# A weight gradient by block products of pairs on one core: stores, the second slice's load, the last visit and the order of work are changed

## The chip, the cores and the metric

The kernel runs on one core of a Trainium2 chip. Its time is what the device measures for one execution, in microseconds: the median of three runs before the change is 161.35 us (161.24 to 161.46). One execution was also profiled.

## What is computed

```python
def reference(input, grad_output):          # (16, 512, 1024), (16, 512, 768), float32
    grad_weight = np.einsum('bmk,bmn->kn', input, grad_output)
    return grad_weight.astype(np.float32)   # (1024, 768)
```

Batch and m together are 8192 rows: the result is X^T G, X of 8192 x 1024 and G of 8192 x 768.

## The kernel before, in words

**Slices and pairs.** The 8192 rows are 64 slices of 128 rows. K is cut into two halves of 512 columns, each of four blocks q of 128, and N into two halves of 384 columns (LEFT, RIGHT). The first eight slices (`LOADS`, kind "s") are multiplied directly: four products A, B (left half of K by LEFT and RIGHT) and C, D (right half of K), each with four blocks q. The other 56 slices are taken in 28 pairs (kind "P", numbers 4 to 31): a pair is a 2 x 2 block product, done by seven products, A, B, C, 1, 5, 6, 7, in place of eight. Their operands are partly the data (A, 1, B, C), partly sums of halves in bf16 that VectorE makes (`sum_x`, `sum_g`, three stages each: tokens x0.u, x1.u, x2.u, g0.u, g1.u, g2.u). Every matmul is 128 x 128 stationary by 384 columns in bf16; there are 4 x (3 x 36 + 8 + 4 x 28) = 912.

**Loads.** Slices from the third on, and G from the second on, are loaded by GpSimd's software queue, which converts float32 to bf16 on the way. To begin early, X of slices 0 and 1 (`xf[0]`, `xf[1]`) and G of slice 0 (`gf`) come as float32 on the hardware queues of SP and ACT (lines 128 to 131) and are rounded to bf16 by VectorE and ACT (`round_by`, line 202). The roundings of G's right half and of slice 1 are tokens r0 to r4: r0 G RIGHT, r1 X columns 512 to 767, r2 X columns 0 to 255 (all on VectorE), r3 X columns 768 to 1023, r4 X columns 256 to 511 (on ACT).

**Visits.** PSUM has eight banks, and 32 blocks (p, q) are to be summed, so that most blocks visit a bank many times. "B0@2.1" opens a visit of block B0 in bank 2 with one matmul, "B0.3" goes on with three; "A0@R.1" uses the bank that A0, A1 or A2 holds for most of the run (5, 6, 7). A visit ends with a close: c by ACT (a copy, line 356), v by VectorE (a copy on the first visit, line 376, else bank plus the sum so far, line 378), k by VectorE with D folded in. "fB2@4" fills bank 4 with B2's sum so far by an ACT copy (line 309), and the matmuls add to it; a suffix s takes the sum from an aside. p and q are sums by GpSimd (line 388) in which a shared product is added.

**End.** A, B and C are finished by adding a shared product (line 371, or q by GpSimd), D by the last close of product 5, which does two sums (lines 364 and 366). Each of the 16 finished blocks of 128 x 384 is stored by `store` (line 291); with `HALVED = 4` the first four stores are cut in two halves each. A fill with two banks ("fB2@7+1") splits a visit in columns 0 to 255 in the first bank and 256 to 383 in the second; then `multiply` runs all its matmuls on the first part and then all on the second, and the last close does one sum and one store for each part, the first on SP's queue, the second on ACT's (lines 372 and 373). The order before has no such visit.

**Order.** `PLAN` is a list of such tokens in program order. Each engine takes its own instructions strictly in that order, and semaphores make it wait for its data and for its bank. SP issues the stores in the same order. Before TensorE's first real matmul, `WARMUP` runs matmuls on constants: one of 512 columns in bf16, two of 512 in float32, and fourteen of 128 columns in bf16.

Of the kernel before, what the change touches and what calls it, by code (L numbers as in the profile page):

```python
# [9 lines left out]
P = 128  # L10
# [4 lines left out]
    "C0@2.1 A0@R.1 r0 r1 r3 B1@1.1 r2 A2@R.1 r4 A1@R.1 vB1 A1.1 D3@4.2 A0.1 C0.1 D0@3.1 B2@0.1 cC0 B2.1 D0.1 "  # L15
    "fB1@1 A2.1 B3@2.2 cD3 B1.2 B3.1 D2@4.1 cB1 D2.1 vB3 D2.1 D0.1 A0.1 C1@2.3 C2@1.4 A1.2 cC2 B2.1 C1.1 B2.1 "
    "D2.1 cC1 D1@1.2 vD2 D1.1 fD3@2 D1.1 A2.2 cD0 vD1 B0@4.1 D3.2 A3@3.2 cD3 A3.2 B0.2 vA3 B0.1 C3@1.4 B2.2 "
    "B1@3.1 B0.1 cB2 B0.1 A1.2 cB0 D2@0.2 A0.3 D0@2.3 C3.2 A2.1 C0@4.1 vC3 C0.3 B1.2 B3@1.5 B1.1 D0.1 C0.1 vB1 "
    "C0.1 A0.2 vB3 D0.1 fD3@3 D2.2 vC0 fC3@1 A2.3 vD0 fD1@4 D3.3 vD2 D3.1 D1.1 g0.4 D1.1 fC1@0 D1.2 C3.1 fA3@2 "
    "g1.4 C3.1 C1.1 vD1 cD3 C1.3 kC3 fC2@3 A3.2 g2.4 A3.1 fB2@1 A3.1 x0.4 A3.1 C2.2 cA3 C2.1 x1.4 C2.2 A2.1 "  # L20
    "x2.4 10@2.1 cC2 A0.1 C1.1 v10 12@4.1 60@3.1 cC1 B2.1 g0.5 B2.1 c12 B2.1 61@0.1 g1.5 c60 62@2.1 B0@4.1 vB2 "
    "B0.1 c61 B0.1 11@3.1 c62 A1.1 vB0 A1.1 f12@1 A1.1 13@0.1 x0.5 13.1 12.1 11.1 c13 73@4.1 x1.5 73.1 c11 "
    "50@2.2 c12 k73 51@0.1 53@3.1 c50 53.1 x2.5 A1.1 52@4.1 g0.6 c53 52.1 51.1 fB1@2 A0.1 v52 63@1.2 c51 "
    "71@3.1 g1.6 71.1 fC0@4 g2.5 B1.2 g2.6 B1.1 c63 70@0.1 k71 70.1 C0.1 f10@1 C0.1 x0.6 C0.1 c70 B3@3.2 A1.1 "
    "cC0 10.1 x1.6 10.1 cB1 72@0.1 vB3 72.1 c10 72.1 C1@4.1 x2.6 f62@3 C1.1 60@2.1 k72 60.1 cC1 61@1.2 g0.7 "
    "A0.1 fB2@4 62.1 v61 62.1 B0@0.2 c62 g1.7 B2.2 vB0 c60 C3@1.2 cB2 C3.1 g2.7 C2@3.2 x0.7 fA3@2 C2.1 12@0.1 "
    "f51@4 12.1 vC3 A3.2 cC2 A3.1 v12 51.2 cA3 70@1.1 x1.7 70.1 c51 53@0.1 g0.8 53.1 A2.1 c70 A2.1 x2.7 A2.1 "
    "fB3@2 A1.1 v53 63@4.1 fB1@1 63.1 B3.1 g1.8 B3.1 f11@3 13@0.1 v63 13.1 cB3 B1.2 g2.8 11.1 v13 C3@4.1 cB1 "
    "C3.1 A2.1 x0.8 fC1@2s 11.2 C0@1.1 f71@0 C0.1 vC3 C1.2 cC0 71.1 x1.8 71.1 c11 71.1 vC1 52@1.2 c71 52.1 "
    "g0.9 A1.1 f73@3 60@4.2 v52 50@2.1 f62@0 50.1 g1.9 50.1 f13@1 73.1 v60 73.2 c50 62.1 x2.8 62.1 72@4.1 g2.9 "  # L30
    "72.1 c62 10@2.1 x0.9 10.1 c73 10.1 13.2 f70@0s v10 A0.2 f51@3 A0.1 v72 70.2 c13 51.1 x1.9 51.1 fC2@4s "
    "61@2.1 v70 61.1 fB2@1 61.1 C2.1 x2.9 C2.1 c51 B0@0.1 g0.10 B0.1 c61 B0.1 B2.1 vC2 B2.1 f11@3 B2.1 A2.1 "
    "vB0 f71@4 A3@2.2 x0.10 A3.1 cB2 11.1 A0.1 f12@0 11.1 g1.10 A2.1 71.1 f63@1 vA3 71.1 12.1 c11 12.1 g2.10 "
    "12.1 x1.10 c71 A1.2 g0.11 63.1 c12 63.2 fB1@4 x2.10 C1@3.2 g1.11 c63 62@2.2 vC1 B1.2 fB3@1 B1.1 v62 "
    "C0@0.1 fC3@3 C0.1 B3.1 g2.11 B3.1 cB1 B3.1 x0.11 C3.2 f72@4 C3.1 vC0 13@2.2 cC3 A2.1 x1.11 72.1 cB3 72.1 "
    "v13 72.1 f50@3s 73@0.2 g0.12 73.1 f53@1 52@2.2 v73 52.1 c72 50.2 g1.12 50.1 f60@0s 53.1 v52 53.1 fC0@4s "
    "53.2 g2.12 60.1 f51@2 v50 60.2 c53 A1.1 x0.12 A0.2 fB2@3 A1.1 C0.1 v60 f10@1 51.3 x1.12 C0.1 f70@0 10.2 "
    "vC0 c51 10.1 70.2 g0.13 70.1 f61@4s C2@2.2 x2.12 c70 C2.1 61.1 x2.11 c10 61.2 vC2 B2.2 f11@1 B2.1 g1.13 "
    "B0@0.1 f12@2 v61 B0.2 11.2 vB0 f62@4 11.1 12.2 cB2 x0.13 12.1 A3@0.1 c11 A3.2 g2.13 C1@3.1 f71@1 x1.13 "
    "C1.2 vA3 62.1 c12 62.2 g0.14 71.1 f63@0 71.2 x2.13 fC3@2 A2.1 63.1 vC1 63.1 c71 63.1 C3.1 g1.14 C3.1 c63 "  # L40
    "A2.1 g2.14 B3@1.1 c62 B3.2 x0.14 C3.1 A0.2 cC3 vB3 53@4.3 fB1@2 x1.14 73@0.2 v53 73.1 f72@1 50@3.2 x2.14 "
    "50.1 B1.1 v73 72.3 v50 60@4.2 c72 60.1 g0.15 B1.1 f52@0 B1.2 v60 13@3.3 A1.1 f70@4 x0.15 A1.2 cB1 52.2 "
    "v13 52.2 70.1 g1.15 70.1 c52 x1.15 70.1 A2.1 fC2@3 A2.1 g2.15 C0@0.1 g0.16 C0.1 c70 C0.1 C2.1 fB2@2 x2.15 "
    "C2.2 vC0 B0@4.2 cC2 B2.1 g1.16 B2.2 fC1@3 g2.16 51@1.2 vB0 51.1 cB2 12@0.2 x0.16 12.1 f10@4 C1.3 v51 10.2 "
    "cC1 10.1 x1.16 10.1 61@2.1 v12 61.1 c10 61.2 x2.16 f11@1 A1.1 71@0.1 g0.17 71.1 fB3@4 71.1 v61 62@3.3 v71 "
    "B3.3 v62 53@2.2 cB3 B1@0.1 g1.17 B1.1 11.1 v53 11.3 vB1 f60@2 A3@4.3 x0.17 c11 A3.1 A2.1 f72@3 A2.1 vA3 "
    "50@0.1 70@1.2 g0.18 72.1 f13@4 72.1 50.1 x1.17 50.1 72.1 v70 13.2 c72 13.1 g1.18 60.2 g2.17 c13 60.1 v50 "
    "63@1.1 fB2@3 63.2 g2.18 63.1 f73@0 A0.1 x0.18 A0.1 f52@4 A0.2 73.1 c60 x1.18 73.2 x2.17 73.1 52.1 x2.18 "
    "63.1 c73 C0@2.2 v63 C0.1 B0@0.2 vC0 B0.2 52.1 g0.19 52.1 fA3@2 A1.2 vB0 c52 B2.3 g1.19 f61@4 10@1.1 x0.19 "
    "10.2 A3.2 g2.19 51@0.2 x1.19 cA3 51.2 v10 cB2 A2.1 61.2 f62@2 v51 61.1 C1@3.2 x2.19 fC2@0 C1.1 62.1 g0.20 "  # L50
    "62.2 B1@1.1 vC1 B1.1 c62 C2.1 g1.20 B1.1 f53@3 A2.1 A1.1 g2.20 12@2.1 c61 vB1 12.3 f11@4 x0.20 C2.2 f70@1 "
    "C2.1 53.1 v12 53.1 cC2 53.2 x1.20 11.2 v53 A2.1 70.1 c11 70.1 x2.20 70.1 fB0@3 52@2.1 g0.21 52.1 B2@0.1 "
    "c70 B2.1 B3@4.1 g1.21 B3.1 v52 B3.2 B0.1 vB2 B0.1 C3@1.2 g2.21 C3.1 fC2@0 C3.1 vB3 C3.1 cB0 C3.2 A0.1 "
    "f72@2 A0.1 vC3 A0.1 13@4.1 C2.1 x0.21 13.1 f50@1 13.2 71@3.1 g0.22 71.2 x1.21 71.2 g1.22 72.3 g2.22 72.1 "
    "v71 50.2 c72 50.2 C2.1 x0.22 fC1@2 C2.1 13.1 A1.1 f60@3 A1.1 x1.22 A1.1 cC2 C1.2 v13 c50 C1.1 60.1 x2.21 "
    "60.1 cC1 60.1 x2.22 60.1 f63@0 60.1 C0@1.2 v60 C0.2 63.1 g0.23 63.3 vC0 A0.1 B0@3.1 c63 B0.1 g1.23 61@4.1 "
    "f51@1 61.2 x0.23 62@0.1 f11@2 62.1 51.1 vB0 51.3 x1.23 11.2 v61 11.2 61@3.1 A0.1 A2.1 v61 A2.2 62.1 v11 "
    "62.1 73@4.2 g0.24 f70@2 73.3 x2.23 c51 10@3.2 v62 10.1 fA3@1 10.2 x0.24 A1.2 70.2 x1.24 70.2 v10 50@0.3 "
    "x2.24 A3.2 v50 A3.3 v73 B1@3.1 fB3@0 B1.2 g2.23 cA3 B1.1 g0.25 B1.1 c70 B3.2 vB1 B3.1 f13@1 B3.1 12@2.1 "
    "g1.25 f53@4 12.2 x0.25 12.1 f52@3 12.1 53.2 vB3 53.2 x1.25 53.1 13.2 v12 13.1 52.1 g1.24 52.1 c13 52.1 "  # L60
    "g2.25 52.1 c53 52.1 x2.25 63@2.1 A0.1 f11@0 g0.26 63.2 B2@1.1 g1.26 11.2 v63 A2.2 B2.2 f60@2 x0.26 B2.2 "
    "c11 A0.1 B0@4.1 c52 B0.1 x1.26 B0.1 60.1 g2.24 fC2@0 60.1 g2.26 60.2 71@3.2 g0.27 c60 71.1 C2.2 x2.26 "
    "C2.2 vB0 C3@2.1 B2.1 A1.1 g1.27 fC0@4 A1.1 kC2 C3.3 g2.27 C3.1 f72@0 C0.2 x0.27 C0.3 vC3 71.3 kC0 72.1 "
    "fC1@2 72.2 vB2 72.1 fA3@4 72.2 x1.27 C1.2 c72 v71 C1.3 g0.28 f73@0 62@1.3 fB3@3 kC1 62.1 A0.1 73.1 g1.28 "
    "73.1 f51@2 v62 73.2 A3.1 g2.28 A3.2 x0.28 A3.1 52@1.2 cA3 51.1 x2.27 51.1 c73 51.1 x1.28 51.2 52.1 A1.1 "
    "50@0.1 v52 50.3 v51 61@4.1 f70@1 61.2 g0.29 61.2 70.1 g1.29 70.2 v61 70.1 A2.1 A1.1 v50 B3.1 f63@4 12@2.2 "
    "x0.29 12.1 63.3 x1.29 A2.2 g2.29 A2.1 70.1 x2.28 63.1 A0.1 v12 A0.2 B3.1 k70 B3.2 B1@0.1 x2.29 B1.1 cB3 "
    "B1.1 g0.30 B1.1 c63 B1.1 10@2.2 x0.30 f60@4 10.4 vB1 60.2 53@3.1 g1.30 53.2 x1.30 53.2 g2.30 13@0.2 v53 "
    "13.2 60.2 g0.31 f72@3 A1.2 f11@1 v10 A0.1 A2.1 72.1 g1.31 72.1 f12@2 72.1 11.1 g2.31 11.1 x2.30 11.2 "
    "x0.31 11.2 A1.1 13.1 c11 13.1 x1.31 12.1 cA1 12.1 v13 12.1 A0.1 f62@1 A2.1 x2.31 10@6.1 p63 c12 72.1 60.1 "  # L70
    "v10 cA2 62.3 cA0 62.1 v60 63@7.1 f73@6 63.1 qA0 v62 A3@0.1 f70@4 A3.1 73.1 v63 73.1 f50@5 73.2 qA2 v72 "
    "70.1 f53@2 A3.1 50.1 v73 70.1 fC3@3 53.1 50.1 v70 f61@1 qA1 50.1 C3.2 v53 fC2@7 C3.2 fB3@6 C3.1 pA3 61.2 "
    "cC3 61.1 v50 C2.1 f71@4 C2.3 qC3 f51@3 C2.1 v61 71.2 cC2 71.1 vA3 71.1 fC0@1 B3.1 qC2 B3.1 v71 B3.1 fB1@7 "
    "51.2 vB3 f52@0 51.1 C0.1 pC1 C0.1 fB0@4 v51 C0.2 fB2@5 C1@2.4 vC0 B1.2 52.1 vC1 52.2 vB1 B2.3 v52 B2.2 "
    "B0.4 vB2 B0.2 vB0 "
).split()

WARMUP = [("b", 512), ("f", 512), ("f", 512)] + 14 * [("b", 128)]
PAIRS_HELD = 11
SUMS_HELD = 8  # L80
MERGED = 2
HALVED = 4
ASIDES = 7
# [5 lines left out]
def kernel(  # L89
# [6 lines left out]
    nc = tc.nc  # L96
    bf16 = mybir.dt.bfloat16
    f32 = mybir.dt.float32
# [242 lines left out]
    def close(engine, p, q, queue):  # L341
# [39 lines left out]
        if last(p, q) and not opened[p, q] and not (engine == "c" and p in "ABC"):  # L381
            closed.add((p, q))
# [66 lines left out]
```

## Time and profile before

| what | value |
| --- | --- |
| median of three runs | 161.35 us (161.24 to 161.46) |
| the profiled execution, its own time | 161.48 us |
| its span in the trace | 159.7 us |
| mean granted TensorE clock | 0.999 |
| TensorE (PE) busy | 154.6 us (97%) |
| VectorE (DVE) busy | 136.1 us (85%) |
| ScalarE (ACT) busy | 104.4 us (65%) |
| GpSimd (POOL) busy | 42.6 us (27%) |
| DMA mean, software queue's share of it | 209 GB/s, 90.7% of 16 engines' span |
| first real matmul, sixth, last (start) | 5.91, 7.70, 155.75 us |
| last store issued, landed | 156.70, 158.80 us |

The span is from the first instruction to the last; the time of the execution holds 1.8 us more around it. Busy times of one engine overlap with those of others, so that they do not add up. A line of a timeline gives start, busy time, engine, line of the kernel, operation, what it writes and reads, how many such instructions were merged, and in brackets how long the engine was idle before and what ended that. Queue q0 is GpSimd's software queue, q1 is SP's and q10 ACT's.

### The profile page before, as it was taken

The numbers are of one execution on the slowest core, as the hardware profiler recorded it, in microseconds if no ns is written. First come the engines' busy times: TensorE is split into PE (matmuls) and PEld (weight loads), VectorE is DVE, ScalarE is ACT, GpSimd is POOL, SyncE is SP. The second block draws the span as 40 slices with busy tenths as digits, with TensorE's granted clock in tenths as the row PEclk, the third lists the DMA queues.
The fourth block names the chain that finished last, engine by engine and source line by source line (L and its number), as shares of the span: only waits on it lengthen the run. The fifth ranks groups of instructions, "written<-read, shape, count | busy, mean of one in ns | idle before, by whom it ended". The sixth has DMA issues, their size and how long they took to land.

```text
span 159.7 us, 2734 instructions
## 1 busy us (share of the span) xinstructions
PE 154.6 (97%) x931; PEld 91.2 (57%) x931; DVE 136.1 (85%) x316; ACT 104.4 (65%) x243; POOL 42.6 (27%) x77
## 2 busy tenths in 40 slices
PE   8899999999999999999999999999999999999990
PEld 3456656556555565665656565656566565656560
DVE  0514169999999999999999999989999899999992
ACT  3445238999999999967867585563465472339930
POOL 7442222222212222221222221222222100006930
PEclk9999999999999999999999999999999999999999
DMA  5999999999999999999999999999999999940696
GB/s 171 297 212 211 214 216 212 213 213 212 213 213 211 214 212 213 214 211 214 213 214 212 214 213 214 212 211 213 213 211 219 208 214 213 213 81 0 196 353 239
DMA packets 12829, 33.40 MB, mean 209 GB/s; under 512 B 1424, under 2 KB 4624, under 8 KB 12816
## 3 DMA queue, kind: packets, MB, share of 16 engines
q0 software_dynamic: 9360, 28.64, 90.7%
q1 hardware_dynamic: 3168, 3.54, 6.6%
q10 hardware_dynamic: 288, 1.05, 1.7%
q8 instruction: 7, 0.11, 0.3%
q14 instruction: 6, 0.05, 0.1%
HBM read 58.72 MB, written 3.15 MB: 387 GB/s over the span
## 4 chain that ended last, share of the span: by engine, by line
PE 91%; DMA 4%; DVE 2%; issue 1%; ACT 0%; ACTq 0%; DVEq 0%
PE bank L331 91%; DMA xf<-in_input_dram 4%; DVE acc L371 1%; DVE macc L364 0%; DVE xp L202 0%; ACT macc L356 0%; ACTq L129 0%; DVE acc L378 0%; DVE acc L366 0%; DVEq L371 0%
## 5 line engine op out<-in xcount | busy, mean ns | idle before, releaser
L331 PE MATMUL bank<-gp,xp 128*128 128x384 bf16 x576 | 105.4, 326 | 0.7 <-DVE xp L202 0.6
L331 PEld LDWEIGHTS <-xp 128*128 128x128 bf16 x576 | 55.8, 98 | 39.1 <-DVE xp L202 1.0
L331 PE MATMUL bank<-ge,xe 128*128 128x384 bf16 x336 | 65.9, 326 | 0.0
L331 PEld LDWEIGHTS <-xe 128*128 128x128 bf16 x336 | 32.7, 98 | 22.3 <-DVE xe L184 0.6
L309 ACT COPY bank<-macc 128x384 f32<-128x384 f32 x69 | 32.6, 489 | 10.4 <-DVE macc L378 6.2
L356 ACT COPY macc<-bank 128x384 f32<-128x384 f32 x64 | 29.4, 484 | 10.4 <-PE bank L331 10.1
L378 DVE TENSOR_TENSOR macc<-bank,macc 128x384 f32<-128x384 f32 x56 | 30.5, 554 | 1.2 <-PE bank L331 0.9
L154 POOL DMA_DIRECT2D xp<-in_input_dram x30 | 15.9, 529 | 52.6 <-DMA xp<-in_input_dram 21.9
L309 ACT COPY bank<-acc 128x384 f32<-128x384 f32 x46 | 21.8, 485 | 11.5 <-DVE acc L378 8.9
L356 ACT COPY acc<-bank 128x384 f32<-128x384 f32 x44 | 20.7, 480 | 11.4 <-PE bank L331 11.1
L153 POOL DMA_DIRECT2D gp<-in_grad_output_dram x30 | 15.9, 531 | 38.4 <-PE bank L331 17.2
L378 DVE TENSOR_TENSOR acc<-bank,acc 128x384 f32<-128x384 f32 x42 | 22.8, 553 | 1.9 <-PE bank L331 1.9
L184 DVE TENSOR_TENSOR xe<-xp 128x1024 bf16<-128x1024 bf16 x28 | 19.3, 689 | 1.0 <-DMA xp<-in_input_dram 0.9
L194 DVE TENSOR_TENSOR ge<-gp 128x768 bf16<-128x768 bf16 x28 | 15.5, 552 | 0.2 <-DMA gp<-in_grad_output_dram 0.2
L376 DVE COPY acc<-bank 128x384 f32<-128x384 f32 x9 | 5.0, 555 | 8.9 <-PE bank L331 8.9
L186 DVE TENSOR_TENSOR xe<-xe,xp 128x512 bf16<-128x512 bf16 x28 | 11.8, 421 | 0.3
L188 DVE TENSOR_TENSOR xp<-xp,xe 128x512 bf16<-128x512 bf16 x28 | 11.5, 419 | 0.0
L196 DVE TENSOR_TENSOR ge<-gp,ge 128x384 bf16<-128x384 bf16 x28 | 9.9, 353 | 0.2
L198 DVE TENSOR_TENSOR gp<-ge,gp 128x384 bf16<-128x384 bf16 x28 | 9.8, 354 | 0.2
L388 POOL TENSOR_TENSOR acc<-acc,macc 128x384 f32<-128x384 f32 x7 | 6.8, 1003 | 0.5 <-ACT acc L356 0.5
L388 POOL TENSOR_TENSOR macc<-macc 128x384 f32<-128x384 f32 x1 | 1.0, 1042 | 18.0 <-DVE macc L378 18.0
L202 DVE CAST gp<-gf 128x192 bf16<-128x192 f32 (+1 forms) x2 | 0.6, 310 | 4.9 <-DMA gf<-in_grad_output_dram 4.9
(23 smaller groups left out, 41.2 us busy)
## 6 DMA issues: line engine op xcount, KB each, us to landing
xp<-in_input_dram POOLq DMA_DIRECT2D x30, 512.0 KB, 16.7
gp<-in_grad_output_dram POOLq DMA_DIRECT2D x30, 384.0 KB, 16.7
out_dram<-acc SPq DMA_DIRECT2D x12, 192.0 KB, 2.1
xf<-in_input_dram ACTq DMA_DIRECT2D x2, 512.0 KB, 4.9
out_dram<-acc SPq DMA_DIRECT2D x8, 96.0 KB, 1.7
gp<-in_grad_output_dram POOLq DMA_DIRECT2D x3, 192.0 KB, 6.4
xp<-in_input_dram POOLq DMA_DIRECT2D x2, 256.0 KB, 7.8
gf<-in_grad_output_dram SPq DMA_DIRECT2D x2, 192.0 KB, 4.1
```

What stands on the lines that cost most here:

```text
L153: nc.gpsimd.dma_start(out=gp, in_=G[rows, :].rearrange("(p m) n -> p m n", m=2))
L154: nc.gpsimd.dma_start(out=xp, in_=X[rows, :].rearrange("(p m) k -> p m k", m=2))
L184: nc.vector.tensor_sub(out=xe[:, 0:2, :], in0=x[:, 1::-1, :], in1=x[:, 3::-2, :])
L186: nc.vector.tensor_sub(out=xe[:, 2, :], in0=xe[:, 0, :], in1=x[:, 0, :])
L188: nc.vector.tensor_add(out=x[:, 1, :], in0=x[:, 2, :], in1=xe[:, 2, :])
L194: nc.vector.tensor_add(out=ge[:, 0:2, :], in0=g[:, 0:2, :], in1=g[:, 1::2, :])
L196: nc.vector.tensor_add(out=ge[:, 2, :], in0=g[:, 3, :], in1=ge[:, 0, :])
L198: nc.vector.tensor_add(out=g[:, 1, :], in0=ge[:, 2, :], in1=g[:, 2, :])
L309: nc.scalar.copy(out=tile_[:, at : at + c1 - c0], in_=src[:, c0:c1])
L331: nc.tensor.matmul(tile_[:, at : at + c1 - c0], stat, mov[:, c0:c1], start=fresh, stop=True, skip_group_check=True,)
L356: nc.scalar.copy(out=to, in_=b)
L378: nc.vector.tensor_add(out=to, in0=b, in1=to)
```

## The change

Five parts, in the words of the code:

- `HALVED` is 0: every store of a whole block is one transfer.
- X of slice 1 is loaded in four transfers of 256 columns (1 KB a row) in place of one (4 KB a row): columns 512 to 767 and then 0 to 255 on SP's queue behind both halves of `gf`, columns 768 to 1023 and then 256 to 511 on ACT's queue behind `xf[0]`.
- The first warm-up matmul writes bank 4, the others bank 7 (all wrote bank 7).
- `PLAN` is another order of the same 912 matmuls. It has 128 visits that open a bank (127 before), 119 closes by c (115), 117 fills (115), 128 closes by v (129), two p and six q (three and five). Its first and last lines are below. B2's last visit is "fB2@7+1", with 2 and then 5 matmuls, and its close is the last token.
- `close` may now end a prepared block by ACT and store it; the new order has no such close.

```diff
 PLAN = (
-    "C0@2.1 A0@R.1 r0 r1 r3 B1@1.1 r2 A2@R.1 r4 A1@R.1 vB1 A1.1 D3@4.2 A0.1 C0.1 D0@3.1 B2@0.1 cC0 B2.1 D0.1 "
...
-    "cC3 61.1 v50 C2.1 f71@4 C2.3 qC3 f51@3 C2.1 v61 71.2 cC2 71.1 vA3 71.1 fC0@1 B3.1 qC2 B3.1 v71 B3.1 fB1@7 "
-    "51.2 vB3 f52@0 51.1 C0.1 pC1 C0.1 fB0@4 v51 C0.2 fB2@5 C1@2.4 vC0 B1.2 52.1 vC1 52.2 vB1 B2.3 v52 B2.2 "
-    "B0.4 vB2 B0.2 vB0 "
+    "A0@R.1 C2@2.1 A3@3.1 A2@R.1 cC2 A1@R.1 vA3 C0@1.1 C1@0.1 vC1 r3 r0 r2 D2@4.1 r1 D2.1 vC0 B0@2.2 B1@0.2 "
+    "cB0 D1@1.2 r4 C3@3.3 D2.1 A1.1 cC3 A1.1 vD2 A2.1 cB1 A2.1 B3@2.2 fC1@0 B3.1 C0@3.2 fA3@4 C1.2 vC0 C1.1 "
...
+    "f72@6 61.1 qA2 61.1 v70 50.1 cA0 50.2 f52@0 v61 53.1 72.1 fB3@7 72.1 qC0 v50 72.2 fC3@3 52.2 B3.1 f71@5 "
+    "B3.1 v72 qA0 C3.1 fC2@2 C3.2 v53 C3.1 cB3 C3.1 71.1 f51@4 71.1 qB3 71.1 v52 cC3 71.2 C2.1 fB2@7+1 C2.2 "
+    "qC3 C2.1 v71 C2.1 fC1@0 51.2 vC2 fB1@3 51.1 C1.2 v51 fB0@6 C1.2 B1.2 B0.2 vB1 B0.3 vC1 B0.1 B2.2 vB0 B2.5 "
+    "vB2 "
 ).split()
-HALVED = 4
+HALVED = 0
-    nc.scalar.dma_start(out=xf[1], in_=X[P : 2 * P, :])
-
-    wps = psum.tile([P, 512], f32, name="bank7")
-    for dt, cols in WARMUP:
+    for engine, b in ((nc.sync, 4), (nc.scalar, 6), (nc.sync, 0), (nc.scalar, 2)):
+        cols = slice(b * P, (b + 2) * P)
+        engine.dma_start(out=xf[1][:, cols], in_=X[P : 2 * P, cols])
+
+    for n, (dt, cols) in enumerate(WARMUP):
         dtype = f32 if dt == "f" else bf16
+        wps = psum.tile([P, 512], f32, name="bank4" if n == 0 else "bank7")
         nc.tensor.matmul(
...
             if engine == "c":
                 assert carried or away
                 assert not final or p in "ABC"
+                assert (p, q) not in prepared or (final and carried and len(parts) == 1)
                 nc.scalar.copy(out=to, in_=b)
...
         if final and p in "ABCD" and engine == "v" and (len(parts) == 1 or p == "A"):
             store(p, q, 0, NH, queue)
-        if last(p, q) and not opened[p, q] and not (engine == "c" and p in "ABC"):
+        if final and engine == "c" and (p, q) in prepared:
+            store(p, q, 0, NH, queue)
+        if last(p, q) and not opened[p, q] and (engine != "c" or p not in "ABC" or (p, q) in prepared):
             closed.add((p, q))
```

## The prediction, as it was put on record

> **What bounds the kernel now.** I read the page's slices first, then the chain of waits in order of time, then the timelines of the first 16 us and the last 8 us, then the DMA rows of short windows and the landing time of each load.
>
> The slices (4 us each), three rows of busy tenths:
>
> ```profile
> PE   8899999999999999999999999999999999999990
> DVE  0514169999999999999999999989999899999992
> DMA  5999999999999999999999999999999999940696
> ```
>
> TensorE, VectorE and the DMA engines are all full from 20 us to about 138 us. No one engine can be relieved for a large gain; only edges and small stalls are left. The chain says whose edges:
>
> ```profile
> 7.70 80.68 PE bank L331 x493
> 88.38 0.03 issue
> 88.41 0.49 ACT macc L356
> 88.90 0.04 issue
> 88.94 64.87 PE bank L331 x397
> ...
> 156.12 0.56 DVE acc L371
> ```
>
> From 7.70 us on it is TensorE, with one eviction in between, and at the end one VectorE sum. Matmuls of 384 columns start 0.1625 us apart. I call "the line" 7.70 + 0.1625 x (k - 6) for the k-th of the 912: a TensorE that never waits after the 6th. The last matmul starts at 155.75, 0.85 us behind the line. That 0.85 is all that the middle can give back.
>
> The loads pace it too. By the landings, a new X pair arrives every 4.3 us, and the pair's first matmul follows after 0.1 to 2.2 us (pair 6: 34.22 and 34.3; pair 10: 51.75 and 51.8; pair 31: 142.53 and 143.2). A TensorE that starts earlier meets data that is not there.
>
> The head, in the timeline:
>
> ```profile
> 4.57 1.50 PE L136 MATMUL bank<-const-bfloat16-1.0 128*128 128x128 bf16 x14
> 5.91 1.17 PE L331 MATMUL bank<-gp,xp 128*128 128x384 bf16 x5
> 6.02 0.36 DVE L202 CAST gp<-gf 128x384 bf16<-128x384 f32 x1 [0.71 <-DMA gf<-in_grad_output_dram]
> 7.14 0.50 DVE L202 CAST xp<-xf 128x256 bf16<-128x256 f32 x2 [0.76 <-DMA xf<-in_input_dram]
> 7.55 0.55 DVE L376 COPY acc<-bank 128x384 f32<-128x384 f32 x1
> ```
>
> Warm-ups keep TensorE until 5.91, five matmuls of slice 0 follow, then it waits for slice 1's X (landed 7.12) and its rounding; the sixth starts at 7.70.
>
> The tail, timeline and DMA issues of the page:
>
> ```profile
> 155.55 1.13 DVE L371 TENSOR_TENSOR acc<-bank,macc 128x384 f32<-128x384 f32 x2
> 155.75 0.33 PE L331 MATMUL bank<-gp,xp 128*128 128x384 bf16 x1
> 156.12 0.91 SPq L291 DMA_DIRECT2D out_dram<-acc  x2
> out_dram<-acc SPq DMA_DIRECT2D x12, 192.0 KB, 2.1
> out_dram<-acc SPq DMA_DIRECT2D x8, 96.0 KB, 1.7
> ```
>
> Call T the end of the last matmul's streaming, 155.75 + 0.16 = 155.92. The last sum starts at T + 0.20, ends at 156.68 (T + 0.76), its store is issued at 156.70 and lands at 158.80 (T + 2.88); 0.91 us of closing work follows. Stores of 192 KB land 0.52 to 0.57 us apart (mean 0.535) from 152.9 to the end: the write stream is full.
>
> **The head after the change.** The new order has seven matmuls of slice 0 that need only the left half of g (A0 C2 A3 A2 A1 C0 C1), then D2 on slices 0 and 1, B0 twice, B1 twice, and D1 as the 14th. The warm-ups are the same, so the first again starts at 5.91 and the seventh at 6.89. On VectorE the eviction vC1 stands before the rounding r0 of g's right half. vC1 can start 0.36 us after its matmul (as 155.75 to 156.12), at 7.25; evictions follow at 0.465 us (the tail's sums), so r0 runs 7.72 to 8.08 (0.36, row above) and the eighth matmul starts at 8.13. The line has it at 8.02. Then r2 (X columns 0 to 255), r1 and vC0 come on VectorE, each behind the other, and D1 needs the bank that vC0 frees.
>
> So it matters when r2's quarter lands, second on SP's queue behind both halves of g and another quarter. How do queues share the engines? Two windows, 2.75 to 3.5 us and 5.25 to 6.5 us (queue; packets, MB, share):
>
> ```profile
> q10 hardware_dynamic: 54, 0.22, 71.6%
> q1 hardware_dynamic: 52, 0.08, 28.2%
> ...
> q10 hardware_dynamic: 73, 0.26, 56.0%
> q0 software_dynamic: 76, 0.12, 52.0%
> ```
>
> Packets alternate one for one, whatever their size (4096 against 1536 bytes). A whole X row is one packet of 4096 bytes; a quarter's is 1024. So against the software queue (137 ns a packet) slice 1 now moves 1 KB a turn on each of two queues instead of 4 KB on one. A 1536-byte packet takes 65 ns, one of 4096 bytes 159: by the straight line through both, 46 to 48 ns for 1024 bytes. The new transfers follow on their queues with pauses of 0.25 to 0.45 us (as between the two gf loads, and the two xf loads). Eight packets per engine and quarter, in turns: until 4.8 with the right half of g (0.065 + 0.046 = 0.11 us a turn), from 5.3 with the software queue (0.137 + 2 x 0.048 = 0.23 us a turn of three queues, 0.185 of two). ACT's first quarter is through at 5.0, SP's first at 6.4, ACT's second at 7.15, SP's second at 8.3, landing 0.2 to 0.4 later (as xf: data through 6.5, landing 6.55 to 7.12 over the engines): about 8.5. I take 8.5; ends 7.1 (as now) and 9.0 (every pause long). Then r2 starts at 8.5, r1 at 8.7, vC0 at 8.9, done 9.47, D1 at 9.53, **0.52 us behind the line** (0.1 to 1.0). The second issue on ACT (0.45 us) delays its table load from 1.67 to 2.1, done 3.4, before its first data at 4.22: nothing. SP's two more issues precede any store: nothing.
>
> [...]
>
> **The load stream.** 512 packets at 46 ns instead of 128 at 159 are 3.2 us of engine time, 0.2 us over 16 engines, and pauses before the software queue starts (5.25) leave some 0.1 us idle. All software loads come 0.3 us later (0.1 to 0.45). In the new order pair 31's first matmul is the 834th (835th now), on the line at 142.23; landing 142.53 + 0.06 + 0.3 puts TensorE at least 0.66 behind. Pairs 9 and 20 ask for 0.6. So the head's 0.52 is covered, and the end of the middle lies between 0.66 and that plus stalls of other kinds. Before had 0.15 (40.4 us) and 0.25 (88.9 us, the eviction in the chain); part of such stalls is absorbed by the wait for loads. I take 0.80, against 0.85 now: **-0.05** (-0.4 to +0.6). The counts of copies change by 4 more evictions and 2 more fills on ACT, 0.41 us each beside work on an engine busy 65%: nothing. VectorE has one eviction fewer.
>
> **The tail.** The last visit, B2, has 7 matmuls, each now one of 256 and one of 128 columns with a weight load each. The warm-ups are the row: 128 columns take 1.50/14 = 0.107 us. 256 columns lie between that and 0.1625; I take 0.11, by the streamed columns. Cost 7 x (0.11 + 0.107 - 0.1625) = **+0.38** (0 if 128 columns took a third of 0.1625; 0.75 if 256 took 0.1625).
>
> [...]
>
> VectorE meanwhile is free: after B1, C1 and B0 (sums at T - 2.3, T - 1.8, T - 1.3) it takes the 256 columns at T - 0.33 and the 128 at T + 0.20. The 384-column sum lasts 0.56, the smallest cast 0.23; I take 0.29 for 128 columns. The store of 64 KB goes out on ACT's idle queue: an unhindered 96 KB one took 1.64, of which data is 0.3; 64 KB, 1.57. It lands at T + 0.2 + 0.29 + 0.03 + 1.57 = T + 2.09, against T + 2.88: **-0.79** (-0.5 to -0.9). The 128 KB part, issued at T + 0.1, is down before that unless the write stream is backed up.
>
> Four stores fewer on SP: its 20 issues stood 0.49 us apart from 147.2 to 154.9 and held the stream at 204 GB/s until 152, against 366 after. In the new order the last seven whole stores become ready 0.4 to 0.6 us apart; the backlog of 0.2 us that the last store now carries is in the -0.79.
>
> **Sum.** Against the profiled execution: 161.48 - 0.05 + 0.38 - 0.79 = 161.02. Its time stands 0.13 above the median of the runs; from 161.35 the forecast is **160.9**.
>
> **Rivals.**
> *The quarters land early.* If the 1 KB packets are not held to one a turn, the head is 0.1 behind and loads come 0.1 late; TensorE ends 0.5 behind the line, -0.35, with the tail 160.6. Against it: the counts of the windows. Chance 0.15.
>
> *The middle takes it back.* In the new order 23 visits open a bank no more than 7 matmuls after its last user's (19 now, of which one stalled, 0.25), and VectorE is full. Two or three more stalls of 0.2 that loads do not absorb: 161.35 +- 0.25. Chance 0.22. With 0.05 for the tail's gain being eaten by backed-up writes (161.2).
>
> *Bank handovers on a late VectorE, slower.* The same place; it decides from five such stalls on: head 0.52 + 1.1 = 1.6 behind the line, +0.77 - 0.41: 161.7. For it: head and order leave VectorE no pause after 8 us. Against it: before, with as full a VectorE, had two. Chance 0.18.
>
> **Numbers.** Forecast 160.9 (160.7 to 161.1), chance 0.40; early quarters 0.15: faster 0.55. Same 0.27, slower 0.18; 0.2% (0.32 us) is about what a measurement here can tell from no change. The range takes in the early head with a free split, 161.35 - 0.4 - 0.8 = 160.15, and a late head with stalls, 161.35 + 0.6 - 0.1 = 161.85.
>
> **What would show it.** The eighth matmul near 8.1 and the 14th near 9.5; casts of r2 waiting for xf until 8.5; pair 31 landing near 142.8; the last seven pairs of matmuls 0.22 us a pair; last VectorE sum about 0.3 us, last landing near T + 2.1 on ACT's queue. I am wrong if the 14th starts at 9.1 or at 10, if 128 columns take 0.054, or if TensorE's idle time in the middle grows past 1 us.

## The result, and the profile after

The changed kernel takes 166.78 us (median of six runs, 164.77 to 167.44) against 161.31: 1.029 times as long, with an interval of 1.023 to 1.035. I had forecast 160.9 and a range up to 161.85. Its profiled execution is the longest of the six (167.44 us, span 165.6) and is compared below with the profiled 161.48 of before. That execution counts as a slow run, 1.6% above the fastest of the six, and the ratio leaves it out and goes by the means of the runs, 166.01 against 161.35. Its mean granted clock is 1.000; the other five, which left no trace, have 0.979 to 0.990.

The chain of waits of the changed kernel, in order of time (start, us, what):

```profile
0.78 2.31 PE bank L138 x3
3.09 0.04 issue
3.13 2.09 PE bank L138 x2
5.22 0.04 issue
5.26 0.28 PE bank L138
5.54 0.04 issue
5.58 0.28 PE bank L138
...
9.69 2.25 PE bank L333 x7
11.94 0.02 issue
11.96 0.56 DVE acc L379
12.52 0.28 DVE gp L204
12.84 148.76 PE bank L333 x907
161.60 0.02 issue
161.63 0.42 DVE acc L374
```

In the chain of before, the first 7 us belonged to a load. Here they belong to the warm-ups (line 138), one by one: each lasts 0.28, then 0.04 of issue, then the next. Two lines of the timeline say the same in bulk:

```profile
5.26 4.42 PE L138 MATMUL bank<-const-bfloat16-1.0 128*128 128x128 bf16 x14
...
9.48 2.44 PE L333 MATMUL bank<-gp,xp 128*128 128x384 bf16 x7
```

Fourteen warm-ups that took 1.50 us now take 4.42, and the first real matmul starts at 9.48 instead of 5.91. The seven real matmuls behind it take 2.44 us: they start 0.32 apart, twice the 0.1625 of before, and so do the next ones up to 16.3 us.

The account of TensorE, from the starts of its matmuls. The 19th starts at 16.30, where the line of the prediction has 9.81: 6.49 us behind. That is 3.57 of later start, 0.95 for six steps at 0.32, 1.28 of waiting before the eighth (r0 behind vC1), 1.67 for eleven more slow steps, less the 0.98 that the first matmul of before is ahead of the line. From the 19th to the end only 0.13 is lost. The end of the matmuls is then 161.71 against 155.92: 6.49 + 0.13 + 0.02 (the split) - 0.85 = 5.79 later (the pace, not rounded, is 0.16248). Nearly all of the loss lies before 16.3 us.

The tail, in the timeline of the last microseconds:

```profile
160.31 1.07 DVE L374 TENSOR_TENSOR acc<-bank,macc 128x384 f32<-128x384 f32 x2
...
160.76 1.88 SPq L293 DMA_DIRECT2D out_dram<-acc  x4
161.63 0.62 DVE L374 TENSOR_TENSOR acc<-bank,macc 128x256 f32<-128x256 f32 x2 [0.25 <-PE bank L333]
162.28 0.37 ACTq L293 DMA_DIRECT2D out_dram<-acc  x1
```

The last sum is short, as forecast (128 columns in 0.28), and ends at 162.25, T + 0.54 with T = 161.71. But SP issues its stores back to back, 0.49 apart, to the end, each landing 0.43 to 0.56 after the one ahead. ACT's small store, issued at 162.28, lands at 164.67, 2.4 us later: T + 2.96. Before it was T + 2.88.

### The profile page after: what moved, and what is told of

Its sections match the earlier page's. It is cut to its first block, busy times and chain, and to the rows that moved or that the text cites. A ratio compares the mean times of both kernels' runs of the same rounds, so it can differ in the third digit from the quotient of the medians.

```text
span 165.6 us, 2754 instructions
## 1 busy us (share of the span) xinstructions
PE 159.3 (96%) x938; PEld 93.2 (56%) x938; DVE 136.1 (82%) x316; ACT 107.3 (65%) x250; POOL 42.5 (26%) x77
## 2 busy tenths in 40 slices
DMA packets 12829, 33.40 MB, mean 202 GB/s; under 512 B 1424, under 2 KB 4752, under 8 KB 12816
## 4 chain that ended last, share of the span: by engine, by line
PE 96%; DVE 1%; issue 0%; DVEq 0%
PE bank L333 91%; PE bank L138 5%; DVE acc L379 0%; DVE acc L374 0%; DVE gp L204 0%; DVEq L449 0%
## 5 line engine op out<-in xcount | busy, mean ns | idle before, releaser
L333 PE MATMUL bank<-gp,xp 128*128 128x384 bf16 (+2 forms) x583 | 107.2, 330 | 0.9 <-DVE gp L204 0.9
L333 PEld LDWEIGHTS <-xp 128*128 128x128 bf16 x583 | 57.6, 99 | 40.1 <-issue 4.6
L333 PE MATMUL bank<-ge,xe 128*128 128x384 bf16 x336 | 64.9, 326 | 0.0
L311 ACT COPY bank<-macc 128x384 f32<-128x384 f32 x66 | 31.3, 488 | 11.0 <-DVE macc L381 6.8
L359 ACT COPY acc<-bank 128x384 f32<-128x384 f32 x50 | 23.3, 482 | 17.1 <-PE bank L333 17.0
L381 DVE TENSOR_TENSOR macc<-bank,macc 128x384 f32<-128x384 f32 x59 | 32.2, 554 | 2.4 <-PE bank L333 1.8
L311 ACT COPY bank<-acc 128x384 f32<-128x384 f32 (+2 forms) x52 | 24.6, 482 | 12.4 <-DVE macc L381 7.1
L381 DVE TENSOR_TENSOR acc<-bank,acc 128x384 f32<-128x384 f32 x40 | 21.9, 555 | 7.7 <-PE bank L333 7.3
L138 PE MATMUL bank<-const-bfloat16-1.0 128*128 128x128 bf16 (+1 forms) x15 | 4.3, 286 | 1.6 <-PEq L438 0.8
L138 PEld LDWEIGHTS <-const-bfloat16-1.0 128*128 128x128 bf16 x15 | 1.6, 109 | 4.8 <-issue 4.8
```

The costliest lines, as they stand in the source:

```text
L138: nc.tensor.matmul(wps[:, 0:cols], nc.const_aps.tensor(1.0, (P, P), dtype), nc.const_aps.tensor(1.0, (P, cols), dtype), start=True, stop=True,
L311: nc.scalar.copy(out=tile_[:, at : at + c1 - c0], in_=src[:, c0:c1])
L333: nc.tensor.matmul(tile_[:, at : at + c1 - c0], stat, mov[:, c0:c1], start=fresh, stop=True, skip_group_check=True,)
L359: nc.scalar.copy(out=to, in_=b)
L381: nc.vector.tensor_add(out=to, in0=b, in1=to)
```

## The experiments

Theory 1 after seeing this: the edit of the warm-up lines gives every warm-up a new PSUM tile in the same bank, and a new tile waits until the matmul that wrote the old one has ended (0.28 us, then 0.04 of issue, in the chain above). In the instruction list of the compiled kernel before, no warm-up waits; in that of the changed kernel each one from the third on does:

```
Matmult bank_86<-const-float32-1.0 128x512
Matmult bank_88<-const-float32-1.0 128x512 [waits PE_49]
Ldweights const-bfloat16-1.0
Matmult bank_90<-const-bfloat16-1.0 128x128 [waits PE_49]
```

Theory 2: the new order and the quartered load are a loss by themselves.

**e1_one_tile**, one tile ahead of the loop, all else changed:

```diff
-    for n, (dt, cols) in enumerate(WARMUP):
-        wps = psum.tile([P, 512], f32, name="bank4" if n == 0 else "bank7")
+    wps = psum.tile([P, 512], f32, name="bank7")
+    for dt, cols in WARMUP:
```

> The changed kernel with one edit: the warm-ups write one PSUM tile, allocated ahead of the loop, as before. Theory 1 (a tile per warm-up makes each warm-up wait for the one ahead; that costs the 3.6 us of later start and the half-speed matmuls until 16 us): fourteen warm-ups 0.107 us apart, first real matmul at 5.91, real matmuls 0.1625 apart from the first. Then the rest of the change shows: SP's second quarter lands at 9.8 as in the changed kernel, D1 (the 14th) starts near 10.8, loads 0.4 to 1.0 later than before: 162.0 to 162.8. Theory 2 (the new order and the quarters are the loss): still above 164.

Measured: 163.76 (162.67, 162.82, 164.71, 164.86) against 161.42 of before on the same chip, ratio 1.015 (1.008 to 1.021). The profiled execution is the 162.67. Its timeline:

```profile
4.57 1.29 PE L138 MATMUL bank<-const-bfloat16-1.0 128*128 128x128 bf16 x14
...
5.70 1.30 PE L333 MATMUL bank<-gp,xp 128*128 128x384 bf16 x7
...
7.91 0.77 PE L333 MATMUL bank<-gp,xp 128*128 128x384 bf16 x3 [0.92 <-DVE gp L204]
9.74 0.50 DVE L204 CAST xp<-xf 128x256 bf16<-128x256 f32 x2 [1.89 <-DMA xf<-in_input_dram]
...
10.09 1.15 PE L333 MATMUL bank<-gp,xp 128*128 128x384 bf16 x5 [1.41 <-DVE xp L204]
```

The warm-ups are quick again, real matmuls start at 5.70 at full speed, and the 14th starts at 10.76 as expected. Theory 1 holds for the largest part. The remaining 1.2 to 3.4 us are the rest of the change: VectorE's cast waits for the last quarter until 9.74, and TensorE with it.

**e2_before_tile_each**, the kernel before with only the reverse edit, and **e3_two_tiles**, the changed kernel with bank 4 kept for the first warm-up but one tile for the others:

```diff
+        if n < 2:
             wps = psum.tile([P, 512], f32, name="bank4" if n == 0 else "bank7")
```

> The kernel before with one edit: a new PSUM tile for each warm-up, the first in bank 4, the others in bank 7. Theory 1: warm-ups 0.32 us apart, first real matmul near 9.5, 0.32 us a matmul until about 16 us: some 5 us slower, 165 to 167. Theory 2: within 0.5 us of before.

> The changed kernel with two warm-up tiles, bank 4 for the first and one in bank 7 for all the others: bank 4 is kept, the tile per warm-up goes. Theory 1 (the new tile, not the bank): as the kernel with one tile, within 0.3 us. Rival (bank 4 itself costs, D2's visit there waits): the 165 of the changed kernel, or a stall at D2.

Measured: 165.08 (163.81 to 165.93), ratio 1.022 (1.017 to 1.028), and 162.92 (162.69 to 164.41). In e2 the fourteen short warm-ups start at 5.26 and the first real matmul at 9.48, as in the changed kernel; the matmuls are 0.32 apart to the 12th (13.0), there to the 19th (16.3). So the tile per warm-up alone costs the old kernel 3.6 us (by the means of the runs). Three runs of e3 take 162.69 to 162.93, as the two quick ones of e1 do (162.67, 162.82), so bank 4 is harmless.

**e4_two_short**, the changed kernel with two 128-column warm-ups, still a tile each:

```diff
-WARMUP = [("b", 512), ("f", 512), ("f", 512)] + 14 * [("b", 128)]
+WARMUP = [("b", 512), ("f", 512), ("f", 512)] + 2 * [("b", 128)]
```

> The changed kernel with 2 warm-ups of 128 columns instead of 14, still a tile each: warm-ups end near 5.9, so the later start is gone and only the half speed is left. Theory 1 with both halves: first real matmul near 5.9, still 0.32 us apart until 11 to 16 us, 163 to 165. Rival (only the delay counts, the speed comes by itself with the first matmuls): full speed before 8 us and the time of the kernel with one tile.

Measured: 164.42 (164.24 to 164.59). Theory 1 was wrong in its second half: matmuls run at full speed from 5.6 on. But they fall back to 0.32 from 11.7 to 14.9, after TensorE has stood idle from 8.5 to 10.3 for the quarter. Three stretches (each with its length, busy times and counts of PE, PEld, DVE, ACT and POOL, then the granted clock, which is the third value from the end):

```profile
5.00:11.40 6.40, 3.56 (x18) 1.58 (x18) 2.80 (x9) 2.20 (x6) 2.06 (x5) 1.00 1.12 224
11.50:14.80 3.30, 3.30 (x12) 1.59 (x11) 0.56 (x1) 1.75 (x4) 1.12 (x3) 0.50 1.11 218
15.00:20.00 5.00, 5.00 (x33) 3.00 (x32) 1.90 (x4) 2.46 (x6) 1.58 (x3) 1.00 1.09 216
```

In the trace's clock records the half speed lasts from 11.49 to 14.90, 3.41 us. Only one execution of each kernel left a trace. By my estimate 3.41 us at half clock lower the mean clock of such a run by 0.010; the four runs of e4 have 0.986 to 0.990 and the two of e1 near 164.8 have 0.985 and 0.987, so they probably all lost it, and e1's two near 162.7 (1.000 and 0.996) did not. So the late quarter cost a second time, by about 2 us (the distance between e1's two pairs), when TensorE lost its clock behind the pause. The length of the pause alone does not decide it: e9b, further down, lost the clock after 2.2 us (7.14 to 9.32), and e16 kept it after 3.1 us (6.71 to 9.81). What decides stays open.

**e5_one_load, e6_halved, e7_unsplit** take the other parts away in turn. e5 is e1 with one load, e6 is e5 with halves, e7 is e5 with one bank for B2:

```diff
-    for engine, b in ((nc.sync, 4), (nc.scalar, 6), (nc.sync, 0), (nc.scalar, 2)):
-        cols = slice(b * P, (b + 2) * P)
-        engine.dma_start(out=xf[1][:, cols], in_=X[P : 2 * P, cols])
+    nc.scalar.dma_start(out=xf[1], in_=X[P : 2 * P, :])
 # e6:  HALVED = 4          e7:  fB2@7 in place of fB2@7+1
```

> The changed kernel with one warm-up tile and X of slice 1 again as one load on ACT's queue: what is left of the change is the order, the whole stores and the split last visit. Theory 1 (warm-up tiles and quarters are all the loss): xf lands near 7.1, D2 starts near 7.9 to 8.1 and D1 near 9.1, loads as before, no second clock record below 1.0; last matmul ends 0.2 to 0.5 earlier than before, but the stores land one after another at 0.53 us and the last lands some 2.9 after it: 161.0 (160.8 to 161.3). Theory 2 (the order is a loss by itself): 161.8 or more.

> The kernel with one tile and one load, and the first four stores halved again. If the end is bound by how fast the last nine stores go out (0.5 us an issue, 0.53 a landing), four more issues at the front cost nothing as long as SP waits for its data between them: within 0.15 of the kernel without halving. Rival (SP's queue is behind from the first store on): 0.5 to 1.0 slower.

> The kernel with one tile and one load, with B2's last visit in one bank. In the changed kernel a 128-column matmul there takes 0.056 and the pair 0.165, so the split costs TensorE nothing. If the write stream sets the end, the split gains nothing either: within 0.15. Rival (the shorter last sum and store do shorten the end, as I forecast): 0.4 to 0.8 slower without the split.

Measured: e5 161.73, ratio 1.0016 (1.0008 to 1.0025); e6 162.53; e7 161.41, ratio 0.9996 (0.9988 to 1.0005). So one load in place of four is worth about 1 us against the quick runs of e1 and about 3 against the others (two chips, so only roughly), and e5 lies between its two theories. Halving costs 0.80 here against what I expected, and the split costs 0.32 where I had expected nothing and forecast a gain. Of the 0.32, the two profiled executions show 0.27 within the span: 0.20 at the end of the matmuls, as the clock is granted at 6.80 in e5 and 6.32 in e7 (the first matmuls run at 0.32), and 0.07 in the stores (last landing T + 2.94 and T + 2.87). The rest lies outside the span: the runs of e5 and e6 have 1.87 to 2.10 us there, those of e1, e7 and the changed kernel 1.72 to 1.85; what this 0.2 is stays open.

The span does not end with the last store's landing. SyncE then goes through waits on the semaphores of its transfers one after another (line 444 in before, 449 in the changed kernel), 0.06 us each and in the order of the program, and how many of them are left behind the last store's own differs from kernel to kernel: from the last landing to the end it is 0.91 us in before, 0.97 in the changed kernel, 1.15 in e7 and 1.34 in e6. This hides a gain: in e7 the matmuls end 0.39 earlier than in before (155.52 against 155.92) and the last store lands 0.41 earlier (158.39 against 158.80), but 0.24 of it goes on these waits.

**e8_before_quarters**, the kernel before with the four quarters:

> The kernel before with only the load of slice 1 in four quarters. Theory 1: the last quarter lands near 9.8, the sixth matmul (A1 on slice 1, columns 0 to 255) starts near 10.3 instead of 7.70, software loads 1.0 to 1.2 later; 163 to 164, and up to 166 where the pause makes TensorE lose its clock. Rival (the quarters are harmless in the old order): within 0.5 of before.

Measured: 165.48 (165.19 to 166.4), ratio 1.026 (1.023 to 1.028). The sixth matmul starts at 10.29, and the profiled execution lost the clock for 3.41 us (11.37 to 14.78). The other three have mean clocks of 0.990, 0.990 and 0.979, so they probably did too. The quarters are as bad in the old order.

**e9b_before_rows**, the kernel before with two loads of 64 whole rows on the two queues:

```diff
+    for engine, r in ((nc.sync, 0), (nc.scalar, 64)):
+        engine.dma_start(out=xf[1][r : r + 64, :], in_=X[P + r : P + r + 64, :])
```

> The kernel before with X of slice 1 in two loads of 64 whole rows (4 KB a row), one on SP's queue behind g and one on ACT's queue. Same two queues as the quarters, but packets of 4 KB. Theory 1 (one packet a turn, so the 1 KB packets are what delays the quarters): both halves land by 6.3 to 6.8, earlier than the single load's 7.1; the sixth matmul starts near 7.5, behind slice 1's g; software loads within 0.2 of before; 161.2 to 161.5. Rival (a second queue and more transfers are the loss): landing after 7.5 and 162 or more.

Measured: 163.58 (162.72 to 166.08). ACT's half landed at 6.63 as expected, SP's at 8.74. The packet size is not the whole reason.

**e11_before_whole** (the kernel before, `HALVED = 0`), **e12_order_alone** (e7 with `HALVED = 4`), **e13_best** (e7 with the loads of e9b, r0 moved ahead, stores of C1 and B0 on ACT):

> The kernel before with only HALVED = 0. Before, the last store waits for VectorE (issued at 156.70 behind a sum that ends at 156.68) and then lands 0.2 later than an unhindered one. Without halves the write stream is less behind: 0.1 to 0.25 faster, 161.2 to 161.4. Rival (whole stores are worth 0.8, as with the new order, where SP's issues ran back to back to the end): 160.7.

> The new order alone: one warm-up tile, one load, B2's last visit in one bank, the first four stores halved as before. With the split last visit, halving cost 0.8. If that is SP's issue pace (20 issues of 0.49 back to back, the new order's stores being ready later or more bunched), it holds here too: 161.9 to 162.3, the order alone a loss of 0.5 to 0.8 that the whole stores win back. Rival (halving costs only together with the split): 161.4.

> What the runs so far point to: new order, one warm-up tile, whole stores, B2 in one bank; X of slice 1 in two loads of 64 rows on the two queues; the rounding r0 of g's right half ahead of the evictions vA3 and vC1; the stores of C1 and B0 on ACT's queue. D2 starts near 7.1 and waits no more for r0. If loads and writes set the pace, nothing is left to win but 0.1 to 0.2 at the last store: 161.1 to 161.4. Rival (the head's 0.4 us and SP's issue pace still count): 160.6 to 161.0.

Measured: e11 161.77, ratio 1.0018 (1.0008 to 1.0027), slower by 0.33 and not faster; e12 161.79, ratio 1.0022 (1.0014 to 1.0031); e13 162.21. In e12 SP issues the last 16 of its 20 stores 0.49 apart without a pause from 149.5 on, and the last goes out at 156.95, 0.39 after the last sum (156.56). So e7 wins 0.38 by whole stores (on another chip), a little less than expected. Its parts are only roughly known: the profiled executions, the longest run of e12 and the shortest of e7, differ by more, 0.28 in the end of the matmuls and 0.67 in the stores (last landing T + 3.54 against T + 2.87), less 0.24 of closing waits. In e11 the last store goes out right behind the last sum, as before, so whole stores had nothing to win. It is slower, and 0.25 of the 0.33 are closing waits (1.16 us against 0.91); its profiled execution, the longest of its ten, also has most loads 0.2 to 0.5 later than before. In e13 the half on SP's queue landed at 8.77, as late as in e9b, and the kernel misses both of its expectations; stores on ACT changed nothing (last landing T + 2.90).

**e15_quarters_act, e16_rows_act**, the kernel before with four quarters, or two loads of 64 rows, all on ACT's queue; **e14_r0_first**, e7 with r0 ahead of vA3 and vC1:

```diff
-... A2@R.1 cC2 A1@R.1 vA3 C0@1.1 C1@0.1 vC1 r3 r0 r2 D2@4.1 ...
+... A2@R.1 r0 cC2 A1@R.1 vA3 C0@1.1 C1@0.1 vC1 r3 r2 D2@4.1 ...
```

> The kernel before with X of slice 1 in four quarters of 256 columns, all four on ACT's queue, the last one columns 256 to 511 and the third 0 to 255. If the 1 KB packets are the loss: 512 packets one a turn behind xf, last landing 9 to 10, 163 to 166. If the place on SP's queue behind g is the loss: last landing before 7.8 and 161.3 to 161.8.

> The kernel before with X of slice 1 in two loads of 64 whole rows, both on ACT's queue: 4 KB packets, the old place, one transfer more. If packet size or SP's place is the loss: landing 7.1 to 7.5, 161.3 to 161.6. If the number of transfers is: 8 or later, 162 or more.

> The new order with one warm-up tile, one load, whole stores and B2 in one bank, and the rounding r0 put ahead of the evictions vA3 and vC1. D2's first matmul then starts at 7.1 to 7.4 instead of 8.4, the second waits for slice 1's g and X (7.5 to 7.8). If loads set the pace from there, 0 to 0.15 faster than without, 161.25 to 161.45; rival (the head's 0.6 us goes through to the end): 160.8 to 161.0.

Measured: e15 165.46 with landings at 6.37, 7.90, 9.55 and 11.03; e16 164.13 (163.1 to 165.52) with landings at 7.09 and 9.17; e14 161.24. In e15 the packets from 6.5 to 9.5 us (queue; packets, MB, share):

```profile
q0 software_dynamic: 281, 0.44, 79.1%
q10 hardware_dynamic: 315, 0.29, 34.2%
```

These counts hold small packets too, 61 of under 512 bytes (in before there are 1424 of these for 89 transfers, 16 for each). The turns are about one for one, and a quarter takes 1.5 us, which is eight turns of 0.137 + 0.05. So the 1 KB packets are a loss here, as I had worked out, and a loss without a second queue too (165.46 against 161.44). In e16, with 4 KB packets, another thing shows, and it is the expectation for the number of transfers that came true. From 5.5 to 6.25 us:

```profile
q0 software_dynamic: 85, 0.13, 92.7%
q10 hardware_dynamic: 12, 0.02, 15.4%
```

The first half is through, the second was issued at 1.73, and yet the hardware queue stands nearly idle until 6.25 while the software queue has the engines. From the mean of the first half's last 16 packets (one on each DMA engine) to the mean of the second half's first 16 are 0.77 us. SP's next transfer paused in the same way at that time: 0.9 us in the changed kernel and in e1, 1.2 in e9b. I had taken 0.25 to 0.45 from pauses ahead of the software queue's start; by this measure the two in before are 0.3 and 0.6. Only the pause that falls in the start of the software queue is long (its first packets run from 5.0 us on): those that began at 5.6 or later took 0.05 to 0.36 (e15, e1 and the changed kernel).

In e14 D2 starts at 7.15 and its second matmul at 7.53, both as expected; against e7 (on another chip) it wins 0.17 of the 0.6 us of earlier order, and against before (161.44, same chip) the ratio is 0.9993 (0.9984 to 1.0002). It is the quickest kernel of this study, and not separable from the one before.

## Why the prediction was wrong, step by step

**"The warm-ups are the same, so the first again starts at 5.91."** This step failed: in the changed kernel the first real matmul starts at 9.48, 3.57 later, and the wait alone costs the old kernel 3.6 us (e2). The warm-ups' list is the same; the line that allocates their tile moved into the loop. I listed the bank edit as a part of the change and never priced it. With a new tile of the same name each warm-up waited for the one ahead to end (0.28 us, then 0.04 of issue), though both are TensorE's own. The trace of before had a 128-column warm-up 0.107 us after the other; with the wait it is 0.32.

**The quarter's landing.** Worked out 8.5, range 7.1 to 9.0; measured 9.8 (e1 and the changed kernel). Turns of one packet each held (e15: 281 packets of the software queue to 315). In the changed kernel SP's first quarter had its last data packet through at 7.41 where the working has 6.4, and the second at 9.27 where it has 8.3. So the second took the 1.9 us of the working, and the 1.0 was lost before. About half of it is the pause ahead of SP's first quarter, the transfer that was next when the software queue started: about 0.9 against 0.25 to 0.45; the rest is not settled. The second landed 0.5 after its last data, where the working has 0.2 to 0.4. What follows had the right mechanism: with 9.74 in place of 8.5, the 14th matmul is expected at 10.8, and e1 has it at 10.76. What no term had is the clock that TensorE lost behind the pause (half speed for 3.41 us in e4 and e8, and by their mean clocks in half of e1's runs too, about 2 us). Spreading slice 1 over two issuing engines brought no gain here: e8 and e9b are 4.0 and 2.1 us slower, though e15, also 4.0 slower, shows that one queue does not save the quarters either.

**The load stream.** Forecast 0.3 later (to 0.45); measured 1.0 to 1.1 for the first loads and for pair 20 (94.89, 95.88 in the changed kernel, 95.99 in e1). With one load, e5, the first loads are 0.3 later. My terms account for 0.3 of the quarters' delay, and no run splits the rest.

**The split.** Forecast +0.38, lower end 0. A 128-column matmul takes 0.056 there and one of 256 0.109: +0.02. The warm-up row that I used was not at full speed: ahead of 5.74 us the warm-ups in that trace start 0.107 apart, from there on 0.06. The page's clock row read full for both, but the clock records begin only at 5.71 us in that trace; before the first record the row says nothing. That the clock was at a half until then is my estimate, from this pace and from the real matmuls 0.32 apart ahead of the first record in the changed kernel.

**The tail.** Forecast -0.79, measured +0.08. The small last sum and store came as worked out, but the store landed 2.4 us after its issue, and the stores ahead of it one by one, 0.43 to 0.56 apart to the end; the small rival "eaten by backed-up writes" describes it, and I had given it 0.05. My walk of the stores had the queue of SP 0.2 behind; it was 0.4 to 0.8 behind for the last seven whole stores, since the stores that wait for GpSimd's sums (about 0.96 apart) hold up the ones after them in SP's order.

**What held.** r0 behind vC1 delays the eighth matmul (1.24 us of step in e1, e5, e7, as 8.13 against 6.89). TensorE ends 0.45 behind the line in e7, against 0.85 before and 0.5 to 0.7 that I had for a kernel bound by its loads; the new order has fewer stalls in the middle. The last store of e7 lands 0.41 earlier than that of before, but 0.24 of it is lost in the closing waits, so that with everything harmful taken out the kernel is at 161.2 to 161.4, not separable from before.

## What to carry to other kernels

Price every line of a diff, also the one that looks like a rename: here an allocation that moved into a loop was a wait for each warm-up from the third on (0.32 us apart in place of 0.107), and it shows in the instruction list before any run. Price a second transfer in a head that is timed to the microsecond: by the medians two loads of 64 rows in place of one cost 2.1 (e9b) and 2.7 us (e16), four quarters 4.0 (e8, e15), and the pause at TensorE's start was paid twice where the clock was lost with it (about 2 us in e1). What is won at the last store is only won when the waits behind it do not grow: in e7 0.24 of 0.41 went there. Before a row is used as a price, check the pace of its neighbours: the clock row of before said 1.00 ahead of its first record at 5.71 us, where the warm-ups were 0.107 apart in place of 0.06.

## What the runs showed of the hardware that was not expected

- TensorE's clock fell to a half for 3.41 us in four traces, 0.4 to 1.2 us after an idle stretch of 1.8 (e4) to 3.4 us (e8), and stayed full after one of 3.1 (e16). With it the late quarter costs e1 3.3 to 3.4 us in two runs, without it 1.2 to 1.4.
- Warm-ups that wait for one another may not bring the full clock: with them it was granted at 16.27 us (changed kernel) and 13.09 (e2), 3.4 and 3.6 us after real matmuls began to run without a break (12.84 and 9.48); without the waits, at 3.9 to 6.8. But e4, whose longer warm-ups wait alike, got it at 4.66, and the five runs of the changed kernel without a trace have mean clocks of 0.979 to 0.990, so this is not settled.
- The pause between two transfers on one hardware queue was 0.2 to 0.7 us while only hardware queues ran, 0.8 to 1.2 us for the one transfer that was next when the software queue started (e16, e1, e9b), and 0.05 to 0.36 behind it (e15, e1 and the changed kernel).
- Behind the last landing SyncE's waits on the semaphores of its transfers take 0.06 us each, and how many are left changes with the transfers of the kernel: 0.91 us from that landing to the end in before, 1.16 in e11, 1.34 in e6.
